# A retention block on one core: earlier loads of the first value weights and of the second chunk's values, another layout of the retention tiles, and another place for some gate products and transpositions

## The chip, the core and the metric

The program runs on one core of a Trainium2 chip. A core has a matrix engine (PE; its weight loads are shown apart as PEld), a vector engine (DVE), a scalar engine (ACT), a general engine (POOL) and a sequencer that issues transfers (SP). Each engine takes its instructions in the order of the program, and waits at semaphores for what other engines or transfers have to deliver. The metric is the device time in microseconds (us) of one execution; smaller is better. All times below are us unless ns is written.

## What is computed

One hybrid decoder block on 1024 tokens of width 1024, batch 1, in float32:

```python
h = modulate(rms_norm(x, norm1_g), sh1, sc1)
proj = h @ w_in                  # retention q, k, v, gate; attention q, k, v; two merge gates
rq, rk = rotary(rq), rotary(rk) * 256 ** -0.5
def step(state, inp):            # retention: 4 heads, 8 chunks of 128 tokens, dk 256, dv 512
    qi, ki, vi = inp
    s = einsum('bhid,bhjd->bhij', qi, ki) * inner_decay
    o = einsum('bhij,bhje->bhie', s, vi) + einsum('bhid,bhde->bhie', qi, state) * q_decay
    state = state * chunk_decay + einsum('bhjd,bhje->bhde', ki * k_decay, vi)
    return state, o
ret_out = (silu(rg) * group_norm(ro)) @ w_ret_out
att_out = merge_by_lse(dilated_group(...) for three groups) @ w_att_out
x = x + g1 * ((sigmoid(gate_a) * ret_out + sigmoid(gate_b) * att_out) @ w_o)
x = x + g2 * (square(relu(modulate(rms_norm(x, norm2_g), sh2, sc2) @ w_ff1)) @ w_ff2)
return rms_norm(x, norm_f_g)
```

## The kernel before

Every product of two float32 matrices is made of three passes of a reduced float32 type: an operand is split into a high half (a rounding copy, mostly on ACT) and a low half (the rest, a subtraction on DVE, or on POOL for the retention's queries and keys), and `mm3` (L196) runs low x high, high x low and high x high into one PSUM tile. So what PE multiplies must have been loaded, copied and subtracted before.

The order of the work is written out by hand; the program's order is the order on each engine. Around the change it is this:

* `queries_keys` (L1152) makes 22 pairs of projections. Each pair is seven block products, in the order `11, s1, s3, s2, 12, 22, s4` (L215), of 12 matmuls each. After a product the function `after` (L1167) issues side work. For the last pair it calls `mod_step` (L1284) at `11` and `12`, which ends in a transfer into the `cossin` tile, and `v_load` (L1208), which issues the loads of the weights of the values' first two products: the first product's after `12`, the second's after `s4`. After `22` it splits the first product's weights: `v_w` (L1215) copies on ACT, `v_low` (L1221) subtracts on DVE.
* `values` (L1291) makes the retention's values in 14 products of four parts each, and writes them to DRAM (`v_d`). Near its end it fetches queries, keys and values of the first chunks, and `first["release"]` lets the weight loader of the steps (`Steps.run`, L71) go on; that loader keeps up to three raw weight tiles (`wraw`, three buffers, tag `raw`) ahead and stops at a mark (`Steps.mark`, L63). Up to here tiles live in the pool `xpool`: 26 buffers of 4 KB for each partition, taken in turn.
* `open_ret` (L520) closes `xpool` and opens the pool `ret` on the same memory. Its tiles are laid out in the order in which their tags are first used: five small tiles (4.5 KB together), `state`, `stateh`, `statel` (4 KB each), four buffers `V` of 4 KB, four buffers `qk` of 2 KB, small ones, three buffers `j` of 4 KB, and so on. A tile's first write waits until the last use of the old tile in the same place is over.
* `chunk` (L723) is one of 32 retention steps, g = 8 h + c. On PE it runs the state's outer product `kv` (6 matmuls), one gate product (`gates`, 6 matmuls of 512 columns, from `rg` weights; not in chunks with c % 4 = 0), the next chunk's scores and transposed keys `s_kt` (L634), the output `o` (3 or 9 matmuls), the transposition `on_T` (L673) of the normalised output of two chunks ago, and the remaining gate products. At the start of chunks with c % 4 = 0 ACT applies `silu` (L719) to the gate of the four chunks before, and then splits queries and keys (`jit_qk`, L623). `s_halves` (L651) copies (ACT) and subtracts (DVE) the transposed keys, `kh` and `kl`; `state` is updated on DVE (L764, L766), its high half `stateh` copied on ACT (L781), its low half `statel` made on DVE (L801). `fetch(g + 3)` at the head of the chunk issues the transfers of queries, keys and values three chunks ahead. PSUM tiles come from two rings: `mm` with two buffers (the gate's sum holds one for four chunks) and `s` with four.

The transfers named here are all issued by SP, in program order, and one that has to wait holds up those behind it. POOL issues its own (`h12d`, L1321 and L1322).

Of the kernel before, what the change touches and what calls it, by code (L numbers as in the profile page):

```python
# [17 lines left out]
P = 128  # L18
# [115 lines left out]
def block_kernel(ctx, tc, io, stop=None, dbg=None):  # L134
# [385 lines left out]
    def open_ret():  # L520
        x_ctx.close()
        R["p"] = ret_ctx.enter_context(tc.tile_pool(name="ret", bufs=1, reuse_waits="tile"))
        for n in R_SMALL:
            R[n] = r_small(n, "00")
        R["state"] = R["p"].tile([P, 2, DV], F32, name="state")
        R["sh"] = R["p"].tile([P, 2, DV], F32R, name="stateh")
        R["sl"] = R["p"].tile([P, 2, DV], F32R, name="statel")
# [4 lines left out]
    def r_small(n, name):  # L532

        if n in R:
            return R.pop(n)
        shape, dt, bufs = R_SMALL[n]
        return R["p"].tile(shape, dt, tag=n, bufs=bufs, name=n + name)

    def etile(name, dt=F32):
        return R["p"].tile([P, 1024], dt, tag="E", bufs=11, name=name)  # L540
# [57 lines left out]
    qk_d = [dram.tile([P, 4, S], F32, name=f"qkd{h}") for h in range(H)]  # L598
    v_d = [dram.tile([P, NC, 2, DV], F32, name=f"vd{h}") for h in range(H)]

    def fetch(i):

        h, c = divmod(i, NC)
        if i > 1:
            hd["qk", i] = R["p"].tile([P, 4, C], F32, tag="qk", bufs=4, name=f"qk{h}{c}")
        elif i == 0:
            t = whl.tile([P, 1024], F32, tag="wl", name="qk01").rearrange("p (a b c) -> p a b c", a=2, b=4)
            for j in range(2):
                hd["qk", j] = t[:, j]
                nc.sync.dma_start(t[:, j], qk_d[0][:, :, j * C:(j + 1) * C])  # L610
        if i > 1:
            nc.sync.dma_start(hd["qk", i], qk_d[h][:, :, c * C:(c + 1) * C])
        if i > 0:
            v = R["p"].tile([P, 2, DV], F32R, tag="V", bufs=4, name=f"v{h}{c}")
        else:
            v = whl.tile([P, 1024], F32R, tag="wh", name="v00").rearrange("p (a b) -> p a b", a=2)
        hd["v", i] = v
        nc.sync.dma_start(fv(v), v_d[h][:, c])

# [3 lines left out]
    def jit_qk(i):  # L623
        src = hd["qk", i]
        if i > 1:
            t = R["p"].tile([P, 2, 4, C], F32R, tag="j", bufs=3, name=f"j{i}")
        else:
            t = whl.tile([P, 1024], F32R, tag=("wh", "wl")[i], name=f"j{i}")
            t = t.rearrange("p (a b c) -> p a b c", a=2, b=4)
        nc.scalar.copy(t[:, 0], src)  # L630
        nc.gpsimd.tensor_sub(t[:, 1], src, fv(t[:, 0]))  # L631
        hd["j", i] = t
# [90 lines left out]
    def chunk(h, c, ahead, w=None):  # L723
        p = R["p"]
        g = NC * h + c
        if g + 3 < NG:
            fetch(g + 3)
        if w:
            hd["w"] = w
        if c in (6, 7):  # L730
            hd["srg", h, c - 4] = etile(f"srg{h}{c - 4}")
            nc.sync.dma_start(hd["srg", h, c - 4], srg_d[h][c - 6])
        if c % 4 == 0:
            if g > 0:
                silu(*divmod(g // 4 - 1, 2))
            hd["rgw"] = hd.pop("w")
            hd["rgp"] = ps_mm(f"rg{h}{c}")
        ks = ((0, 1, 2, 3), (4, 5), (6,), (7,))[c] if g < 4 else range(2 * (c % 4), 2 * (c % 4) + 2)
        early = int(c % 4 > 0)
        gated = h > 0 and 1 < c < 6  # L740

        def gates(ks):
            proj_mm(hd["rgp"], hd["rgw"], ks, (1, 3, 5, 7, 0, 2, 4, 6))

        if g == 0:
            gates(ks[:2])
            s_kt(0)
            s_halves(0)()()
            gates(ks[2:])
        elif g + 2 < NG:  # L750
            jit_qk(g + 2)
        if gated:
            u_scaled(h - 1, c - 2)
        vh, vl = hd["v", g][:, 0], hd["v", g][:, 1]
        st, sh, sl = R["state"], R["sh"], R["sl"]
        if c < NC - 1:
            kh, kl = hd["k", g]
            kv = ps_mm(f"kv{h}{c}")
            for i in range(2):
                mm3([kv[:, i]], (kh[:, i, :], kl[:, i, :]), [(vh, vl)], True, True)  # L760
        if g > 0:
            gates(ks[:early])
        if c == 0:
            nc.vector.tensor_copy(flat(st), flat(kv))  # L764
        elif c < NC - 1:
            nc.vector.scalar_tensor_tensor(flat(st), flat(st), float(GAMMA[h] ** C), flat(kv),  # L766
                                           op0=ALU.mult, op1=ALU.add)
        if g > 0:
            norm_bias(g - 1)
        high = low = None  # L770
        if g + 1 < NG:
            s_kt(g + 1)
            high = s_halves(g + 1)
        po = ps_s(f"o{h}{c}")
        if c > 0:
            t = hd["j", g]
            for i in range(2):
                mm3([po], (t[:, 0, i, :], t[:, 1, i, :]), [(sh[:, i, :], sl[:, i, :])], i == 0, False)
        mm3([po], hd["s", g], [(vh, vl)], c == 0, True)
        if c < NC - 1:  # L780
            nc.scalar.copy(flat(sh), flat(kv if c == 0 else st))  # L781
        if g > 0:
            normed(g - 1)
        if high:
            low = high()
        if g > 1:
            on_T(*divmod(g - 2, NC))
        if g > 0:
            gates(ks[early:])
        bn = p.tile([P, 6], F32, tag="bn", bufs=2, name=f"bn{h}{c}")  # L790
        ba = p.tile([P, 2], F32, tag="ba", bufs=2, name=f"ba{h}{c}")
        gr = p.tile([P, 1], F32, tag="gr", bufs=2, name=f"gr{h}{c}")
        nc.vector.bn_stats(bn, po)
        nc.vector.bn_aggr(ba, bn)
        nc.vector.tensor_add(gr, ba[:, 1:2], ct[:, CS_EPS + h:CS_EPS + h + 1])
        nc.gpsimd.tensor_tensor(gr, gr, mhalf[:, 0:1], op=ALU.pow)
        hd["o", h, c] = po, ba, gr
        if low:
            low()
        if c < NC - 1:  # L800
            nc.vector.tensor_sub(flat(sl), flat(st), fv(flat(sh)))  # L801
        ahead(2)
        if gated:
            u_gated(h - 1, c - 2)
        if g == 0:
            jit_qk(g + 2)
        if g == NG - 1:
            norm_bias(g)
            normed(g)
            silu(h, 1)  # L810

    def wsplit(ap):
        return ap, split_w
# [338 lines left out]
    def queries_keys(ahead):  # L1152
        for _ in range(4):
            copy_block()
        gn_signs()
        sums = [(q, n) for q in range(NA) for n in ORDER][4:]
        while len(BA.slots) > 1:
            BA.prep(sums.pop(0))

        def before(q, n):  # L1160
            if n == ORDER[0] and q + 2 < NA:
                for part in (1, 2):
                    a_load(q + 2, part)

        turns = []

        def after(q, n):  # L1167
            if n in ("s1", "s2", "12"):
                copy_block()
            if n == "11" and 0 < q < 4:  # L1170
                bias_out(q - 1)
            if turns:
                next(turns[0], None)
            if (q, n) == (NA - 6, "22"):
                mod_fetch(0)
                mod_fetch(1)
            if q >= NA - 5 and n in ("11", "12"):
                mod_step()
            if n == ORDER[-1] and PAIRS[q][0] == "r":
                while turns:  # L1180
                    drain(turns.pop())
                turns.append(rotate(q))
            if q == NA - 1 and n in ("12", "s4"):
                v_load(n == "s4")
            if q == NA - 1 and n == "22":
                for j in range(2):
                    v_w(0, j)
                for j in range(2):
                    v_low(0, j)

        BA.run([(q, n) for q in range(NA) for n in ORDER], sums, before, after)
        while turns:
            drain(turns.pop())
        values(ahead)


# [83 lines left out]
    def mod_fetch(i):  # L1280
        if i < len(later_mods):
            nc.sync.dma_start(cs[:, i % 2], io["w_ada"][later_mods[i]])
# [8 lines left out]
    def values(ahead):  # L1291
        last = len(VSEQ) - 1
        for i, (hp, n) in enumerate(VSEQ):
            if i + 2 <= last:
                v_load(i + 2)
            for p in range(4):
# [12 lines left out]
                    mod_step()  # L1309

                if i == last - 2 and p == 2:
                    fetch(0)
                if i == last - 2 and p == 3:
                    first["release"]()
                if i == last - 1 and p in (1, 2):
                    jit_qk(p - 1)
                if i == last - 1 and p == 3:
# [4 lines left out]
                        nc.gpsimd.dma_start(hl[2 * m][:, 512:], h12_d[m][:, 1])  # L1322
        v_post(*V["post"].pop())
        open_ret()
        for g in (1, 2):
            fetch(g)
        banks(False)

    for kk in range(4):
# [9 lines left out]
    for h in range(H):  # L1339
        for c in range(NC):  # L1340
            steps.add((lambda h, c: lambda ahead, *w: chunk(h, c, ahead, *w))(h, c),
                      [wsplit(w) for w in r_loads.get((h, c), ())], manual=True)


    A = {}
# [1339 lines left out]
```

## Time and profile before

| quantity | value |
|---|---|
| median of 3 runs | 2212.76 us (2210.62 to 2216.35) |
| profiled execution | 2214.49 us, span of its trace 2212.6 us |
| PE busy | 2157.9 us, 98% of the span, 10034 matmuls |
| DVE, ACT, POOL busy | 1472.7, 944.8, 169.2 us |
| 568.60 to 725.00, values: PE busy | 154.02 of 156.40 us |
| 725.40 to 960.00, retention: PE busy | 227.64 of 234.60 us |

The profile is one execution. A busy time is the time in which an engine has an instruction under way; idle time ahead of an instruction is put down to what ended last before it started. Positions are us from the start of the span. In the timeline a row is: start, length, engine, line, operation, output<-inputs, shape, count, and in brackets the idle time before it with what ended it. PE's matmul rows overlap: a matmul of 512 columns takes 0.39 us, and the next starts some 0.23 us after it.

### The profile page before, as it was taken

The numbers are of one execution on the slowest core, as the hardware profiler recorded it, in microseconds if no ns is written. First come the engines' busy times: TensorE is split into PE (matmuls) and PEld (weight loads), VectorE is DVE, ScalarE is ACT, GpSimd is POOL, SyncE is SP. The second block draws the span as 40 slices with busy tenths as digits, with TensorE's granted clock in tenths as the row PEclk, the third lists the DMA queues.
The fourth block names the chain that finished last, engine by engine and source line by source line (L and its number), as shares of the span: only waits on it lengthen the run. The fifth ranks groups of instructions, "written<-read, shape, count | busy, mean of one in ns | idle before, by whom it ended". The sixth has DMA issues, their size and how long they took to land.

```text
span 2212.6 us, 27000 instructions
## 1 busy us (share of the span) xinstructions
PE 2157.9 (98%) x10034; PEld 1787.3 (81%) x10034; DVE 1472.7 (67%) x2271; ACT 944.8 (43%) x1709; POOL 169.2 (8%) x176
## 2 busy tenths in 40 slices
PE   7999999999999999999899999999999999999998
PEld 4888888888788788888788788888878888788887
DVE  6756777766566677754555644676876665787855
ACT  4532323333234466654534634524454445533412
POOL 0100111000001233300000000002100000000003
PEclk9999999999999999999999999999999999999999
DMA  9869999744687645569523265654154445645322
GB/s 383 222 208 294 293 304 278 200 153 151 222 298 289 227 158 190 176 216 259 166 79 105 87 214 186 238 179 164 38 191 148 147 147 183 250 135 175 119 86 77
DMA packets 159906, 422.54 MB, mean 191 GB/s; under 512 B 27478, under 2 KB 55389, under 8 KB 155358
## 3 DMA queue, kind: packets, MB, share of 16 engines
q1 hardware_dynamic: 151902, 372.57, 47.5%
q0 software_dynamic: 7872, 48.24, 9.4%
q8 instruction: 79, 1.29, 0.2%
q14 instruction: 53, 0.43, 0.1%
HBM read 325.71 MB, written 160.32 MB: 220 GB/s over the span
## 4 chain that ended last, share of the span: by engine, by line
PE 85%; DVE 6%; ACT 4%; DMA 3%; issue 1%; POOL 0%; SPq 0%; POOLq 0%; DVEq 0%; ACTq 0%
PE qap L200 6%; PE qap L204 6%; PE qap L202 6%; PE fp L200 4%; PE fp L202 4%; PE fp L204 4%; PE f2a L202 2%; PE f2a L204 2%; PE f2a L200 2%; PE ak L200 2%; PE ak L202 2%; PE ak L204 2%; PE va L202 1%; PE va L204 1%; PE va L200 1%; PE rg L202 1%
## 5 line engine op out<-in xcount | busy, mean ns | idle before, releaser
L200 PE MATMUL qap<-hh,qaw 128*128 128x512 f32 x264 | 102.9, 390 | 0.2 <-DVE qat L291 0.2
L202 PE MATMUL qap<-hl,qaw 128*128 128x512 f32 x264 | 102.7, 389 | 0.0
L204 PE MATMUL qap<-hh,qaw 128*128 128x512 f32 x264 | 102.7, 389 | 0.0
L631 POOL TENSOR_TENSOR j<-qk,j 128x512 fp32r<-128x512 f32 x32 | 50.5, 1579 | 326.4 <-ACT j L630 326.4
L2140 ACT ACTIVATE a<-a 128x512 f32<-128x512 f32 x48 | 30.3, 632 | 79.3 <-DVE a L2139 79.3
L2036 POOL TENSOR_TENSOR accnf<-accnf,sqnf 128x256 f32<-128x256 f32 (+1 forms) x18 | 16.6, 922 | 613.3 <-ACT sqnf L2035 613.3
L1492 ACT ACTIVATE P<-P,ng 128x128 f32<-128x128 f32 (+1 forms) x96 | 41.9, 438 | 41.5 <-DVE ng L1489 41.5
L200 PEld LDWEIGHTS qap<-hh,qaw 128*128 128x128 f32 x264 | 49.6, 188 | 11.1 <-DVE qat L291 0.9
L204 PEld LDWEIGHTS qap<-hh,qaw 128*128 128x128 f32 x264 | 49.6, 188 | 10.4
L202 PEld LDWEIGHTS qap<-hl,qaw 128*128 128x128 f32 x264 | 49.6, 188 | 10.3
L2329 ACT CAST w2h<-w2s 128x512 fp32r<-128x512 f32 x36 | 22.4, 622 | 79.0 <-DVE w2s L2367 79.0
L257 DVE TENSOR_TENSOR fw<-w1r,fw 128x512 fp32r<-128x512 f32 x48 | 32.9, 688 | 33.3 <-ACT fw L247 33.3
L257 DVE TENSOR_TENSOR qaw<-wa,qaw 128x512 fp32r<-128x512 f32 x66 | 45.1, 687 | 12.6 <-ACT qaw L247 12.6
L2036 POOL TENSOR_TENSOR accn<-accn,sqn 128x512 f32<-128x512 f32 x12 | 15.6, 1296 | 488.6 <-ACT sqn L2035 488.6
L247 ACT CAST qaw<-wa 128x512 fp32r<-128x512 f32 x66 | 39.8, 617 | 25.3 <-PE qap L204 15.2
L200 PE MATMUL fp<-h2h,fw 128*128 128x512 f32 x128 | 50.0, 390 | 0.0
L204 PE MATMUL fp<-h2h,fw 128*128 128x512 f32 x128 | 49.8, 389 | 0.0
L202 PE MATMUL fp<-h2l,fw 128*128 128x512 f32 x128 | 49.8, 389 | 0.0
L200 PE MATMUL roa<-rh,rwl 128*128 128x512 f32 x128 | 49.8, 389 | 0.0
L202 PE MATMUL roa<-rl,rwh 128*128 128x512 f32 x128 | 49.8, 389 | 0.0
L204 PE MATMUL roa<-rh,rwh 128*128 128x512 f32 x128 | 49.8, 389 | 0.0
L1874 DVE TENSOR_TENSOR rwl<-rwl,rwh 128x1024 fp32r<-128x1024 f32 x25 | 30.2, 1221 | 29.0 <-ACT rwh L1904 29.0
(3057 smaller groups left out, 7126.3 us busy)
## 6 DMA issues: line engine op xcount, KB each, us to landing
cossin<-in_w_ada_dram SPq DMA_DIRECT2D x32, 512.0 KB, 5.1
v<-vd SPq DMA_DIRECT2D x32, 512.0 KB, 4.7
w1r<-in_w_ff_dram SPq DMA_DIRECT2D x32, 512.0 KB, 4.8
vd<-vo SPq DMA_DIRECT2D x24, 512.0 KB, 6.6
yt<-y POOLq DMA_DIRECT2D x6, 2048.0 KB, 15.0
xsd<-as SPq DMA_DIRECT2D x24, 512.0 KB, 3.0
w2r<-in_w_ff2s_dram SPq DMA_DIRECT2D x24, 512.0 KB, 7.6
em<-in_w_ada_dram SPq DMA_DIRECT2D x16, 512.0 KB, 10.2
```

The costliest lines, as they stand in the source:

```text
L200: nc.tensor.matmul(o, wl, xh, start=first, stop=False, skip_group_check=skip)
L202: nc.tensor.matmul(o, wh, xl, start=False, stop=False, skip_group_check=skip)
L204: nc.tensor.matmul(o, wh, xh, start=False, stop=last, skip_group_check=skip)
L247: nc.scalar.copy(t[:, :512], src)
L257: nc.vector.tensor_sub(t[:, 512:], src, fv(t[:, :512]))
L631: nc.gpsimd.tensor_sub(t[:, 1], src, fv(t[:, 0]))
L1492: nc.scalar.activation(v, v, AF.Exp, bias=ng[:, blk:blk + 1], accum_out=st[:, g, blk, 2 + a:3 + a])
L1874: nc.vector.tensor_sub(lo, fv(lo), fv(hi))
L2036: (nc.vector if f == 7 else nc.gpsimd).tensor_add(G["acc", key], G["acc", key], sq)
L2140: nc.scalar.activation(o, o, AF.Relu)
L2329: nc.scalar.copy(hi, src)
```

## The change

Six edits, all around the values and the retention:

1. `v_load` of the first value product moves from behind `12` of the last pair to behind `s1`; that of the second from behind `s4` to behind `12`.
2. `fetch` is split into `fetch_qk` and `fetch_v`. The second chunk's values go into a buffer of `wraw` and are fetched in `values`, right behind the release of the weight loader, and no longer behind `open_ret`. A new mark makes that release stop after two gate weights; a third release at the head of chunk 2 lets the loader go on.
3. Queries and keys are fetched four chunks ahead, values three as before.
4. In `open_ret` a `j` tile is the first tile of the pool, so that the three `j` buffers lie in front and everything else moves up by 12 KB; `qk` now comes ahead of `V`.
5. In chunk 0 the four gate products run one ahead of `s_kt(0)`, one behind it and two behind `o`, in place of two and two.
6. In the chunks with c % 4 = 0 the two gate products at the end run ahead of the transposition, and no longer behind it.

```diff
     def open_ret():
...
+        R["j"] = j_tile(2)
         for n in R_SMALL:
...
+    def j_tile(i):
+        return R["p"].tile([P, 2, 4, C], F32R, tag="j", bufs=3, name=f"j{i}")
...
-    def fetch(i):
+    def fetch_qk(i):
 
         h, c = divmod(i, NC)
         if i > 1:
             hd["qk", i] = R["p"].tile([P, 4, C], F32, tag="qk", bufs=4, name=f"qk{h}{c}")
+            nc.sync.dma_start(hd["qk", i], qk_d[h][:, :, c * C:(c + 1) * C])
...
+    def fetch_v(i):
+
+        h, c = divmod(i, NC)
         if i > 1:
-            nc.sync.dma_start(hd["qk", i], qk_d[h][:, :, c * C:(c + 1) * C])
-        if i > 0:
             v = R["p"].tile([P, 2, DV], F32R, tag="V", bufs=4, name=f"v{h}{c}")
         else:
-            v = whl.tile([P, 1024], F32R, tag="wh", name="v00").rearrange("p (a b) -> p a b", a=2)
+            pool, tag = ((whl, "wh"), (wraw, "raw"))[i]
+            v = pool.tile([P, 1024], F32R, tag=tag, name=f"v0{i}").rearrange("p (a b) -> p a b", a=2)
...
     def jit_qk(i):
         src = hd["qk", i]
         if i > 1:
-            t = R["p"].tile([P, 2, 4, C], F32R, tag="j", bufs=3, name=f"j{i}")
+            t = R.pop("j") if "j" in R else j_tile(i)
...
         if g + 3 < NG:
-            fetch(g + 3)
+            fetch_v(g + 3)
+        if g + 4 < NG:
+            fetch_qk(g + 4)
+        if g == 2:
+            first["release"]()
...
         if g == 0:
-            gates(ks[:2])
+            gates(ks[:1])
             s_kt(0)
             s_halves(0)()()
-            gates(ks[2:])
+            gates(ks[1:2])
...
-        if g > 0:
-            gates(ks[:early])
+        gates(ks[:early])
...
         if high:
             low = high()
+        if c % 4 == 0:
+            gates(ks[early if g else 2:])
         if g > 1:
             on_T(*divmod(g - 2, NC))
-        if g > 0:
+        if c % 4:
             gates(ks[early:])
...
+            if q == NA - 1 and n in ("s1", "12"):
+                v_load(n == "12")
...
-            if q == NA - 1 and n in ("12", "s4"):
-                v_load(n == "s4")
...
                 if i == last - 2 and p == 2:
-                    fetch(0)
+                    fetch_qk(0)
+                    fetch_v(0)
                 if i == last - 2 and p == 3:
                     first["release"]()
+                    fetch_v(1)
...
         open_ret()
-        for g in (1, 2):
-            fetch(g)
+        fetch_qk(2)
+        fetch_v(2)
+        fetch_qk(3)
         banks(False)
...
+            if h == 0 and c == 2:
+                steps.mark()
```

## The prediction

> **What bounds the kernel now.** First the page's head and its busy times, then the waits of PE, then the stages in which these waits lie.
>
> ```profile
> span 2212.6 us, 27000 instructions
> ...
> PE 2157.9 (98%) x10034; PEld 1787.3 (81%) x10034; DVE 1472.7 (67%) x2271; ACT 944.8 (43%) x1709; POOL 169.2 (8%) x176
> ```
>
> PE is busy for 98% of the span, so time can only be won where PE waits, or where its clock is down. The view of the waits of PE, by the instruction that waited, has these rows in the stretch that the change touches (total us, times, longest):
>
> ```profile
> PE oT L680 <- DVE kl L660: 4.1, 4, 1.8
> ...
> PE kv L200 <- DMA v<-vd: 2.8, 1, 2.8
> ...
> PE va L200 <- ACT vwh L1217: 1.6, 1, 1.6
> ...
> PE va L202 <- DVE vwlFalse L1224: 0.8, 1, 0.8
> ```
>
> The view of the windows gives the granted clock (third number from the end):
>
> ```profile
> 560.00:565.00 5.00, 5.00 (x24) 4.14 (x23) 3.81 (x6) 0.60 (x1) 0.00 (x0) 1.00 0.01 3
> 571.60:575.50 3.90, 3.90 (x10) 3.03 (x11) 2.22 (x2) 0.74 (x1) 0.00 (x0) 0.56 0.07 28
> 732.00:734.00 2.00, 2.00 (x14) 1.74 (x12) 0.93 (x1) 0.22 (x1) 0.00 (x0) 1.00 0.04 13
> 1063.60:1070.40 6.80, 3.02 (x8) 2.34 (x9) 3.57 (x8) 6.77 (x10) 0.00 (x0) 0.50 0.89 208
> ...
> 1275.20:1278.60 3.40, 3.40 (x12) 2.92 (x12) 2.04 (x1) 0.18 (x1) 0.00 (x0) 0.50 0.01 5
> 1623.40:1630.20 6.80, 5.73 (x14) 4.47 (x15) 5.58 (x10) 4.43 (x8) 0.00 (x0) 0.50 0.48 177
> ```
>
> Behind the waits at the first value product the clock fell to 0.56 over 3.90 us: 3.90 x 0.44 = 1.7 us lost besides the waiting. Three later places lose 3.4, 1.7 and 3.4 us in the same way.
>
> **First weights sooner (edit 1).** The boundary between the last projection pair and the values, from the timelines of PE, ACT, DVE and SP (`vwlFalse` are the first product's weights, `vwlTrue` the second's):
>
> ```profile
> 568.31 0.39 PE L204 MATMUL qap<-hh,qaw21s 128*128 128x512 f32 x1
> 570.32 0.50 PE L200 MATMUL va<-vwh,hl 128*128 128x512 f32 x1 [1.62 <-ACT vwh L1217]
> 563.35 0.60 ACT L1117 ACTIVATE qa<-qap 128x512 f32<-128x512 f32 x1 [10.30 <-PE qap L204]
> 569.21 1.06 ACT L1217 ACTIVATE vwh<-vwlFalse 128x1024 fp32r<-128x1024 f32 x1 [5.26 <-DMA vwlFalse<-wrv]
> 580.20 1.06 ACT L1217 ACTIVATE vwh<-vwlTrue 128x1024 fp32r<-128x1024 f32 x1 [7.86 <-DMA vwlTrue<-wrv]
> 566.02 1.12 DVE L1119 TENSOR_TENSOR qa<-qap,qat 128x512 f32<-128x512 f32 x1 [1.47 <-PE qap L204]
> 570.30 1.23 DVE L1224 TENSOR_TENSOR vwlFalse<-vwlFalse,vwh 128x1024 fp32r<-128x1024 f32 x1 [3.16 <-ACT vwh L1217]
> 551.56 13.15 SPq L1282 DMA_DIRECT2D cossin<-in_w_ada_dram  x2
> 564.81 0.86 SPq L1213 DMA_DIRECT2D vwlFalse<-wrv  x2
> 567.17 7.81 SPq L1131 DMA_DIRECT2D aqd<-qa  x2
> 575.07 1.22 SPq L1213 DMA_DIRECT2D vwlTrue<-wrv  x2
> ```
>
> The load is issued at 564.81, behind the second `cossin` transfer, and ACT has it at 569.21, 4.4 us later. Issued behind `s1` it stands between the two `cossin` transfers and can leave near 552, if its buffers are free; they are those that the pool would have given to the pair's results. At the pace of the row it is there before 559, and ACT is free at 563.35 + 0.60 = 563.95: two copies of 1.06 end at 566.1. DVE is held until 567.14 by L1119, then needs 1.23 for each low half: 568.4 and 569.6. PE ends the pair at 568.54, wants the first low half one matmul later and the second after six (569.9). So both waits go, 1.62 + 0.76 (0.8 in the waits); each also let PE drain, since a matmul lasts 0.39 but is followed after 0.23 (twelve in 2.72, next fence), 0.16 each; and the 1.7 of the clock. Gain: 2.4 + 0.3 + 1.7 = **4.4 us**. If the buffers come free late, 0 is the other bound; I take 4.4 because the slack in the load is 5 us.
>
> The second product's loads leave at 575.07, behind `aqd`, which waits for DVE, and are split from 580.20. With the values 4.4 us sooner the first product (48 matmuls of 0.227 = 10.9 us) ends at 568.54 + 10.9 = 579.4, and PE would wait 3 us for that second split. Moved ahead of `aqd`, they leave near 565, land by 573 (even at 8 us), and cost nothing: that is the cover for this half of the edit. `aqd` gets 1.2 us behind it on SP and nobody waits for it before the attention.
>
> **Second chunk's values, layout, spread gate products (edits 2, 4, 5).** Rows of PE, DVE and SP:
>
> ```profile
> 725.39 0.61 PE L200 MATMUL rg<-hh,raw_5287l 128*128 128x512 f32 x2
> 728.11 0.28 PE L642 MATMUL sT<-j 128*128 128x256 f32 x1
> 728.67 0.71 PE L200 MATMUL rg<-hh,raw_5287l 128*128 128x512 f32 x2
> 733.98 0.40 PE L204 MATMUL o<-v,smh 128*128 128x512 f32 x1
> 737.16 0.47 PE L200 MATMUL kv<-v,kl 128*128 128x512 f32 x1 [2.78 <-DMA v<-vd]
> 729.52 0.48 DVE L660 SCALAR_TENSOR_TENSOR kl<-kT,ct,kh 128x256 fp32r<-128x256 f32 x1 [1.85 <-ACT kh L659]
> 733.07 1.23 DVE L764 COPY state<-kv 128x1024 f32<-128x1024 f32 x1 [1.90 <-PE kv L204]
> 704.36 2.18 SPq L84 DMA_DIRECT2D raw<-in_w_rg_dram  x3
> 719.53 8.48 SPq L1267 DMA_DIRECT2D vd<-vr  x4
> 733.55 0.32 SPq L618 DMA_DIRECT2D v<-vd  x1
> 780.22 1.22 DVE L191 TENSOR_TENSOR raw_5291l<-raw,raw_5291h 128x1024 fp32r<-128x1024 f32 x1 [0.19 <-ACT raw_5291h L190]
> ```
>
> Two gate products take 728.11 - 725.39 = 2.72, one 1.36; `s_kt` 0.56; `kv`, six matmuls too, 1.36; `o` of chunk 0 0.68. The chunk's work is unchanged in sum. In the new order: gate to 726.75, `s_kt(0)` to 727.31, gate to 728.67. `kl` ended at 730.00, 1.89 behind the start of `s_kt`, so now at 728.64: just in time for `kv` at 728.67 (a spread that cost more would be seen here; up to 0.2). Then `kv`, `s_kt(1)`, `o`, two gates: chunk 1's `kv` is reached at 728.67 + 1.36 + 0.56 + 0.68 + 2.72 = 734.0, and its values now leave SP near 706, in the place of the third `raw` of the row at 704.36. Gain up to 737.16 - 734.0 = 3.1.
>
> But the wait behind the old 733.55 has not gone. The values' transfer stood at the end of the last `vd<-vr` (8.48 from 719.53), with the transfer engines at 13 GB/s by 732-734: it waited for the old tile in its place to be written out. Before, `V` began at 4.5 + 3 x 4 = 16.5 KB; now the three `j` (12 KB) and the small tiles (4.5 KB) put `state` at 16.5 KB, the same place, with `stateh` behind it. So what is late next is DVE's L764, and behind it on DVE `kl` of chunk 1: 733.55 + 1.23 + 0.48 = 735.3, gain 1.9. On ACT `stateh` waits alike, and `jit_qk(2)` behind it; `s_kt(2)` is reached 2.7 us after `kv`, enough for 0.6 on ACT and 1.3 on POOL. One transfer of 512 KB fewer stands ahead of that landing, so it may come a microsecond sooner, or, with queries and values now issued at 728 beside it, some 3 us later (gain -1). Bounds -1 and 3.1; I take **2.3 us**, near the row's 1.9.
>
> The release's mark moves that third gate-weight load and the one behind it to chunk 2, near 744; the third is split at 780.22, so over 30 us cover it. Queries one chunk sooner use buffers last read a chunk earlier, and hide behind everything; three `j`, four `qk` and four `V` remain.
>
> **Transpositions behind the gate products (edit 6).** The four waits of 4.1 us lie at chunks 4, 8, 16 and 24. Chunk 4 from the timelines, and ACT's groups in the retention:
>
> ```profile
> 760.14 0.40 PE L204 MATMUL o<-v,smh 128*128 128x512 f32 x1
> 761.35 0.33 PE L680 MATMUL oT<-ct,onm 128*128 128x128 f32 x1 [0.82 <-DVE kl L660]
> 758.87 1.03 ACT L721 ACTIVATE srg<-rg 128x1024 f32<-128x1024 f32 x1
> L682 ACT COPY on<-oT 128x128 f32<-128x128 f32 x120 | 23.3, 282 | 7.1 <-DVE on L694 6.4 <-PE oT L680 0.7
> L630 ACT CAST j<-qk 128x512 fp32r<-128x512 f32 x30 | 19.0, 634 | 8.1 <-DMA qk<-qkd 8.0
> L689 ACT ACTIVATE on<-on,gnt 128x512 f32<-128x512 f32 x24 | 18.3, 816 | 0.0
> ```
>
> The transposition needs the PSUM buffer that `kl` still reads, and `kl` is late because `silu` stands ahead of it on ACT. Two gate products (2.72) now run in between, more than the longest wait (1.8). They need the `mm` buffer that `silu` reads: free at 759.90, PE there at 760.54. Gain: 4.1 + 4 x 0.16 = **4.8 us**. ACT's copies of the transposition come 2.72 later; behind them wait four copies (1.13), `j` (0.63), and in chunk 5 of a head two L689 (1.63), 3.4 together, while PE needs 1.36 + 1.36 + 0.56 = 3.3 and 0.3 more before the next `kh`: hidden, narrowly.
>
> **Sum.** 4.4 + 2.3 + 4.8 = 11.5 us. The profiled execution took 2214.49 (span 2212.6 and 1.9 around it): 2203.0. It lies 1.7 over the median of the runs shown, about one fall of the clock; from the median it is 2201.3. I predict **2202**.
>
> [...]
>
> **Rivals.** *The clock falls elsewhere* (0.16): everything behind 960 shifts by 11.5 us, and whether a wait lowers the clock depends on more than its length, since the rows above show one fall or two. Two falls more or fewer are 2 x 1.7: 2205.4 or 2198.6. *A wait only moves* (0.10): the transposition still waits behind the gates, or `state` is held for 3 us: 4.8 lost, 2206.8. For it: that landing is unknown; against it: the margins above. *The gain is lost in the attention* (0.05): its waits grow by what was won, 2214.49 - 1.7 = 2212.8. For it: the transfers at 1063.60 (208 GB/s beside a PE busy for 3.02 of 6.80); against it: what they bring is asked for by PE's own progress. *Slower* (0.03): ACT's queue. If the work behind the late copies does not fit, each of the seven chunks 4 to 28 loses up to 2.72: 19.0, 2202 + 19 = 2221. It decides once that work lasts 11.5 / 7 = 1.6 us over the 3.6 that are free; the groups give 3.4.
>
> **Chances.** The forecast has 0.66, with its own range 2199 to 2205. A measurement of this kernel can tell about 0.3%, 6.6 us: faster is below 2206.1, slower above 2219.4. Faster: 0.65 of the forecast, 0.14 of the first rival, 0.03 of the second, 0.82. Slower 0.04, the rest 0.14. The range takes in both signs of the clock and the moved wait: 2197 to 2208.
>
> **What would show it.** No wait of PE at the first `va`, and clock 1.00 there; chunk 1's `kv` 1 to 3 us behind `o` and gates, its wait on DVE; `state<-kv` idle before it on a `vd` transfer; no wait at `oT` in chunks 4, 8, 16, 24. I am wrong if `oT` waits as before, if the first weights leave SP near 564 again, or if waits behind 960 grow by as much.

## The result, and the profile after

The changed kernel takes 2200.71 us (median of 5 runs, 2196.09 to 2206.35) against 2212.76 (5 runs, 2210.62 to 2216.35): the ratio is 0.9943, with a 95% interval from 0.9919 to 0.9966. The forecast was 2202. The profiled execution took 2196.09, the lowest of the five. Its page begins so:

```profile
span 2194.1 us, 26997 instructions
...
PE 2151.7 (98%) x10034; PEld 1784.1 (81%) x10034; DVE 1472.7 (67%) x2271; ACT 944.5 (43%) x1709; POOL 166.4 (8%) x176
```

PE has the same 10034 matmuls. The four rows of PE's waits that the prediction began with (`va` twice, `kv`, `oT`) have no counterpart in the view after. The windows (stretch; its length; busy time of PE, PEld, DVE, ACT and POOL with instructions; clock; DMA share; GB/s) show PE busy all through the two places:

```profile
571.60:575.50 3.90, 3.90 (x19) 3.24 (x18) 2.42 (x3) 2.13 (x3) 0.00 (x0) 1.00 0.90 279
721.00:731.00 10.00, 10.00 (x52) 8.34 (x51) 7.10 (x16) 3.99 (x9) 1.10 (x2) 1.00 1.02 358
...
1608.24:1611.65 3.41, 3.41 (x10) 2.64 (x9) 2.74 (x5) 3.09 (x6) 0.00 (x0) 0.50 0.11 38
```

The last row is the only stretch at half clock between the start and the last six microseconds: 3.4 us, where the execution profiled before had windows of 3.4, 6.8, 3.4 and 6.8 us by the exact edges, 20.5 together. At the clock of 0.50 matmuls of 512 columns start 0.43 us apart (572.18 to 575.17 in the execution before) in place of 0.23, so about half the time is lost at most: by that estimate at most (20.5 - 3.4) / 2 = 8.5 of the 18.4 us between the two profiled executions are the clock's, up to 1.7 of them at the first value product.

The stretches that the change touches can be read directly. From the last matmul of the pair (568.31 before, 569.04 after) to the first gate product of the retention (725.39, 721.59) PE took 157.08 us before and 152.55 after; from there to the attention's first scores (970.36, 958.48) 244.97 and 236.89. That is 4.5 + 8.1 = 12.6 us, of which at most 1.7 are the clock's. The other 5.8 lie outside these stretches: three falls of the clock behind them against one, and one wait at a gate product of the attention of 3.8 us before and 1.6 after. The medians, 12.05 us apart, hold less of that.

The boundary after, from the timelines of PE, ACT, DVE and SP (start; duration; engine; line; operation):

```profile
569.04 0.39 PE L204 MATMUL qap<-hh,qaw21s 128*128 128x512 f32 x1
569.27 0.39 PE L200 MATMUL va<-vwh,hl 128*128 128x512 f32 x1
564.52 2.00 ACT L1230 ACTIVATE vwh<-vwlFalse 128x1024 fp32r<-128x1024 f32 x2
567.82 2.35 DVE L1237 TENSOR_TENSOR vwlFalse<-vwlFalse,vwh 128x1024 fp32r<-128x1024 f32 x2
552.72 1.26 SPq L1226 DMA_DIRECT2D vwlFalse<-wrv  x2
554.02 0.91 SPq L1226 DMA_DIRECT2D vwlTrue<-wrv  x2
565.11 0.33 SPq L1295 DMA_DIRECT2D cossin<-in_w_ada_dram  x1
```

Both products' loads left before the second `cossin`; the copies and low halves were done in time, and PE went from the pair to the values in one matmul's distance, 0.23.

The start of the retention, from the same timelines:

```profile
721.59 0.62 PE L200 MATMUL rg<-hh,raw_5287l 128*128 128x512 f32 x2
726.93 0.48 PE L200 MATMUL o<-v,sml 128*128 128x512 f32 x1
730.02 0.62 PE L204 MATMUL rg<-hh,raw_5287h 128*128 128x512 f32 x2
730.47 0.39 PE L200 MATMUL kv<-v,kl 128*128 128x512 f32 x1
726.58 1.23 DVE L775 COPY state<-kv 128x1024 f32<-128x1024 f32 x1 [0.57 <-PE kv L204]
715.73 8.48 SPq L1280 DMA_DIRECT2D vd<-vr  x4
```

From the first gate product to chunk 1's `kv` PE took 730.47 - 721.59 = 8.88 us, before 737.16 - 725.39 = 11.77: 2.9 won, near the upper bound of 3.1. But DVE's copy into `state` waited for PE's `kv` alone and not for a `vd` transfer, which the prediction named, and chunk 1's `kv` did not wait at all.

At the transpositions, chunk 8 for one, PE ran on (the rows of the four chunks are alike):

```profile
779.56 0.40 PE L204 MATMUL o<-v,smh 128*128 128x512 f32 x1
779.80 0.62 PE L200 MATMUL rg<-hh,raw_5638l 128*128 128x512 f32 x2
...
782.10 0.62 PE L204 MATMUL rg<-hh,raw_5638h 128*128 128x512 f32 x2
782.55 0.60 PE L688 MATMUL oT<-ct,onm 128*128 128x128 f32 x4
```

### The profile page after: what moved, and what is told of

It reads as the page before. It is cut to its first block, busy times and chain, and to the rows that moved or that the text cites. A ratio compares the mean times of both kernels' runs of the same rounds, so it can differ in the third digit from the quotient of the medians.

```text
span 2194.1 us, 26997 instructions
## 1 busy us (share of the span) xinstructions
PE 2151.7 (98%) x10034; PEld 1784.1 (81%) x10034; DVE 1472.7 (67%) x2271; ACT 944.5 (43%) x1709; POOL 166.4 (8%) x176
## 4 chain that ended last, share of the span: by engine, by line
PE 84%; DVE 7%; ACT 4%; DMA 3%; issue 1%; SPq 0%; POOL 0%; POOLq 0%; DVEq 0%; ACTq 0%
PE qap L200 6%; PE qap L204 6%; PE qap L202 6%; PE fp L200 4%; PE fp L202 4%; PE fp L204 4%; PE f2a L202 2%; PE f2a L204 2%; PE f2a L200 2%; PE ak L200 1%; PE ak L202 1%; PE ak L204 1%; PE rg L202 1%; PE rg L200 1%; PE rg L204 1%; PE va L204 1%
## 5 line engine op out<-in xcount | busy, mean ns | idle before, releaser
L200 PEld LDWEIGHTS qap<-hh,qaw 128*128 128x128 f32 x264 | 49.5, 188 | 11.5 <-DVE qat L291 1.4
L257 DVE TENSOR_TENSOR qaw<-wa,qaw 128x512 fp32r<-128x512 f32 x66 | 45.0, 686 | 12.7 <-ACT qaw L247 12.6
L1288 DVE SCALAR_TENSOR_TENSOR cossin<-cossin,cb 128x1024 f32<-128x1024 f32 x32 | 39.0, 1219 | 15.9 <-DMA cossin<-in_w_ada_dram 15.9
## 6 DMA issues: line engine op xcount, KB each, us to landing
em<-in_w_ada_dram SPq DMA_DIRECT2D x16, 512.0 KB, 10.2
```

Of the source, the lines that this page charges most:

```text
L200: nc.tensor.matmul(o, wl, xh, start=first, stop=False, skip_group_check=skip)
L257: nc.vector.tensor_sub(t[:, 512:], src, fv(t[:, :512]))
L1288: nc.vector.scalar_tensor_tensor(t, t, 1.0, cb, op0=ALU.mult, op1=ALU.mult, accum_out=mods[:, j:j + 1])
```

## The experiments

Theory: the three groups of edits remove three waits, each worth what the wait was, and the rest is cover. The rivals: a part does nothing, or does its work through something else, above all through where the last result tile of the values (`vr`) lies. All were run beside the kernel before; since a fall of the clock more or less moves an execution by up to 1.7 us for each 3.41 us at 0.50, the verdict on a part is read from PE's waits, in one profiled execution each. By the times alone no part taken back lies clear of the changed kernel: the intervals all touch or overlap that of changed_again. "Excess" is the distance between two matmuls beyond the usual one of their form, so it holds the wait and the drain of PE.

| run | median us | ratio to before, 95% interval | excess at the places in question |
|---|---|---|---|
| changed_again | 2196.07 | 0.9944 [0.9931, 0.9957] | none |
| first_loads_back | 2199.01 | 0.9949 [0.9937, 0.9961] | `va` 1.68 + 1.03, `sT` of chunk 2 0.47 |
| second_load_back | 2198.25 | 0.9944 [0.9932, 0.9957] | none |
| values_back | 2196.67 | 0.9939 [0.9927, 0.9951] | none |
| layout_back | 2202.04 | 0.9969 [0.9957, 0.9981] | `kv` of chunk 0 3.33 |
| spread_back | 2197.87 | 0.9953 [0.9940, 0.9966] | `kv` of chunk 1 1.19, `sT` of chunk 2 0.58 |
| transpose_first | 2201.84 | 0.9968 [0.9955, 0.9980] | `oT` 0.97 + 0.92 + 0.92 + 0.93 |
| queries_transpose_back | 2201.49 | 0.9961 [0.9949, 0.9973] | `oT` 0.95 + 0.92 + 0.91 + 0.82 |
| fewest_parts | 2196.93 | 0.9942 [0.9928, 0.9956] | none |
| before_first_loads | 2207.90 | 0.9992 [0.9983, 1.0000] | `kv` of chunk 0 2.68, of chunk 1 0.81, `sT` 0.64; `oT` as before |
| before_transpose_behind | 2206.50 | 0.9987 [0.9977, 0.9998] | `va` 2.01 + 1.03, `kv` of chunk 1 2.68 |

The kernel before took 2208.72 to 2209.97 in these sets.

### changed_again

> The changed kernel once more, beside the parts that are taken back. Its ratio to the kernel before should be that of its first measurement, 0.992 to 0.997, and its profile has no wait at va, kv of chunk 1 and oT. Where the profiled execution differs from the first one, theory: only in falls of the clock and in the waits beside them; rival: other waits of PE come and go too.

It held: 13 us below the kernel before, and no wait at the three places. The profiled execution had three falls of the clock (13.7 us at half clock, 0.996 on average over the span) where the first had one (3.4 us, 0.998), and the wait at a gate product of the attention was 2.2 us in place of 1.6 (3.8 in the kernel before).

### first_loads_back: edit 1 taken back

```diff
-            if q == NA - 1 and n in ("s1", "12"):
-                v_load(n == "12")
...
+            if q == NA - 1 and n in ("12", "s4"):
+                v_load(n == "s4")
```

> The changed kernel with edit 1 alone taken back: both products' first value weights are loaded in their old places again, behind 12 and s4; all else stays. Theory: PE waits again at the first va, 1.6 us on ACT's high half and 0.8 us on DVE's low half, with a clock of 0.5 for about 3.4 us behind it in some executions; with the drain of PE that is 2.7 us, 4.4 us where the clock falls. A second effect is to be seen if edit 1 also moved the place of the last result tile of the values (vr of the last block): in this kernel that tile lies under state and stateh, so DVE's copy into state should wait for the landing of the last vd transfer, about 4.4 us after its issue, some 1.7 us longer than in the changed kernel; PE's kv of chunk 1 then stands at most 0.9 us later. Rival: the new layout alone freed state of that wait, and DVE's copy waits for PE's kv only, as in the changed kernel (0.57 us). Time by the theory 2.7 to 5.3 us above the changed kernel.

Two of PE's waits, then rows of DVE, ACT and PE at the start of the retention:

```profile
PE va L200 <- ACT vwh L1230: 1.5, 1, 1.5
...
PE va L202 <- DVE vwlFalse L1237: 0.8, 1, 0.8
```

```profile
724.07 0.61 PE L200 MATMUL rg<-hh,raw_5287l 128*128 128x512 f32 x2
...
730.41 1.22 DVE L775 COPY state<-kv 128x1024 f32<-128x1024 f32 x1 [1.92 <-PE o L204]
731.67 1.01 ACT L792 CAST stateh<-kv 128x1024 fp32r<-128x1024 f32 x1 [1.29 <-DVE state L775]
732.93 0.39 PE L200 MATMUL kv<-v,kl 128*128 128x512 f32 x1
736.12 0.39 PE L650 MATMUL sT<-j 128*128 128x256 f32 x1 [0.30 <-POOL j L639]
```

Both effects are there. The waits at `va` are back, 2.7 us with the drain. And DVE's copy into `state` is idle for 1.92 in place of 0.57: it names PE's `o`, but `kv` had long been done; the last `vd<-vr`, issued at 726.36, landed by the trace at 730.29, and the copy began 0.12 later. So with edit 1 gone `state` does lie on the last result tile, and the prediction's wait exists. It costs little: `kv` of chunk 1 starts 732.93 - 724.07 = 8.86 us behind the first gate product, as in the changed kernel; only `j`, queued on ACT behind the late `stateh`, makes PE wait 0.3 (0.47 with the drain) at `sT` of chunk 2.

### second_load_back: the second product's weights loaded in their old place

```diff
-            if q == NA - 1 and n in ("s1", "12"):
-                v_load(n == "12")
+            if q == NA - 1 and n == "s1":
+                v_load(0)
...
+            if q == NA - 1 and n == "s4":
+                v_load(1)
```

> The changed kernel with the second product's weights loaded behind s4 again, as before the change; the first product's stay early. By the prediction PE would wait 3 us at the second product. By the profile of the changed kernel less: there SP is done with aqd at 571.68, the first of the two loads would land 5.7 to 6.9 us later, near 577.9, its copy (1.06) and low half (1.22) would end at 580.2, just when the first product of 48 x 0.227 = 10.9 us is over (569.27 + 10.9 = 580.2); the second tile 1 to 2 us later, needed 1.4 us later. So 0 to 1 us of waiting, and no fall of the clock. Time 0 to 1 us above the changed kernel by the profile, 3 to 5 us by the prediction.

Rows of SP, ACT and DVE (the tile has the name `vwl` here):

```profile
572.78 1.20 SPq L1228 DMA_DIRECT2D vwl<-wrv  x2
578.18 1.06 ACT L1232 ACTIVATE vwh<-vwl 128x1024 fp32r<-128x1024 f32 x1 [10.54 <-DMA vwl<-wrv]
579.27 1.22 DVE L1239 TENSOR_TENSOR vwl<-vwl,vwh 128x1024 fp32r<-128x1024 f32 x1 [6.96 <-ACT vwh L1232]
```

No wait. The prediction's 3 us fall: it kept the landing of before (580.20), but with DVE done sooner, `aqd` no longer holds SP until 575.07; the load left 2.3 us sooner.

### values_back: chunk 1's values back in the retention's pool

```diff
-        if i > 1:
+        if i > 0:
             v = R["p"].tile([P, 2, DV], F32R, tag="V", ...)
...
-                    fetch_v(1)
...
         open_ret()
+        fetch_v(1)
         fetch_qk(2)
```

> The changed kernel with chunk 1's values back in the retention's own V tile, so that their load is issued only after the pools have changed, behind the last vd transfer on SP. Theory A (the earlier load won the gain): PE waits for them at kv of chunk 1, as before the change, 1 to 3 us. Theory B (the gain came from where the last result tile lies: no tile that is written early in the retention stands on it any more, so SP doesn't hold the load back): the load leaves SP near 724.4, lands near 729 and is there before kv of chunk 1 at 730.5; no wait. By A the time is 1 to 3 us above the changed kernel, by B the same.

```profile
724.62 0.38 SPq L625 DMA_DIRECT2D v<-vd  x1
```

```profile
730.78 0.39 PE L200 MATMUL kv<-v,kl 128*128 128x512 f32 x1
```

Theory B holds: the load left SP right behind the last `vd` (before it was held until 733.55), landed by the trace at 729.39, and PE took it at 730.78 with no wait. Beside edits 1 and 4, loading these values sooner gained nothing.

### layout_back: the old order of the retention's tiles

```diff
         R["p"] = ret_ctx.enter_context(...)
-        R["j"] = j_tile(2)
...
-            t = R.pop("j") if "j" in R else j_tile(i)
+            t = j_tile(i)
```

> The changed kernel without edit 4: the retention's tiles in their old order, the small ones first and j after them. By its addresses the small tiles (sm, kh, kl, smh) and the first part of sml then lie on the last result tile of the values, which the last vd transfer still reads. Theory: ACT's first kh of the retention waits for that landing, which came 6.7 us after the first gate product in the changed kernel; its copy and the low half take 0.5 and 0.5 us more, so kv of chunk 0 starts 7.6 to 8.2 us behind the first gate product in place of 3.4: PE waits 4.2 to 4.8 us, and the clock falls to 0.5 behind it (up to 1.7 us more). Rival: the layout alone is worth nothing, kh waits only for PE's kT, no wait. Time 4 to 6.5 us above the changed kernel by the theory, the same by the rival.

The first copy of the retention on ACT, the wait of PE, and the windows of 3.413 us around it:

```profile
730.75 0.47 ACT L666 ACTIVATE kh<-kT,ct 128x256 fp32r<-128x256 f32 x1 [4.13 <-DMA vd<-vr]
```

```profile
PE kv L200 <- DVE kl L667: 3.2, 1, 3.2
```

```profile
727.33:730.74 3.41, 1.30 (x6) 0.73 (x4) 0.01 (x1) 0.00 (x0) 0.00 (x0) 1.00 0.91 317
730.74:734.16 3.42, 2.36 (x6) 1.88 (x7) 1.26 (x4) 0.93 (x3) 0.00 (x0) 0.50 0.98 313
734.16:737.57 3.41, 3.41 (x13) 2.93 (x12) 2.24 (x5) 1.55 (x4) 0.00 (x0) 0.50 1.05 365
```

The theory's wait, with its releaser named: ACT waits for the `vd` transfer, PE 3.2 us behind it (the landing came sooner than assumed, 3.3 us after its issue), and the clock is at half for two windows. The run is some 6 us above the changed kernel. What the layout does is to put `j` of chunk 2, which is written late, on the tile that is read out last: in the changed kernel ACT writes it from 729.09 on, and the last `vd` had landed by the trace at 728.28.

### spread_back: chunk 0's gate products two and two again

```diff
-            gates(ks[:1])
+            gates(ks[:2])
             s_kt(0)
             s_halves(0)()()
-            gates(ks[1:2])
+            gates(ks[2:])
...
-        if c % 4 == 0:
-            gates(ks[early if g else 2:])
+        if g > 0 and c % 4 == 0:
+            gates(ks[early:])
```

> The changed kernel with edit 5 taken back: chunk 0's four gate products stand two ahead of its s_kt and two ahead of its kv again, and none behind its o. Theory: kv of chunk 1 then comes 0.68 us behind kv of chunk 0 and the 0.56 of s_kt, while DVE needs 1.23 for state and 0.48 for kl after kv of chunk 0 ends: kv of chunk 0 ends near 7.4 us behind the first gate product, kl of chunk 1 near 9.4 and kv would start at 8.6 to 8.9. PE waits 0.5 to 0.8 us at kv of chunk 1. Rival: kl is ahead of PE there too, no wait. Time 0.5 to 1 us above the changed kernel by the theory, the same by the rival.

```profile
731.96 0.50 PE L200 MATMUL kv<-v,kl 128*128 128x512 f32 x1 [1.02 <-ACT stateh L792]
735.41 0.39 PE L650 MATMUL sT<-j 128*128 128x256 f32 x1 [0.42 <-POOL j L639]
```

A wait there is, but it is not `kl`'s: that was done at 730.85 + 0.48 = 731.33. PE waited for ACT's copy out of chunk 0's `kv` (730.90 + 1.01 = 731.91). With the wait at `sT` of chunk 2 behind it, the spread is worth 1.19 + 0.58 = 1.8 us by the waits; the medians differ by as much.

### transpose_first and queries_transpose_back: edit 6 taken back, then edit 3 too

```diff
-        if c % 4 == 0:
-            gates(ks[early if g else 2:])
+        if g == 0:
+            gates(ks[2:])
         if g > 1:
             on_T(*divmod(g - 2, NC))
-        if c % 4:
+        if g > 0:
             gates(ks[early:])
```

> The changed kernel with edit 6 taken back: the transpositions of chunks 4, 8, 12 and so on stand ahead of the second gate products again. Theory: the waits at oT of chunks 4, 8, 16 and 24 return with their sizes of before, 0.8, 0.8, 0.7 and 1.8 us (4.1 together), 4.8 us with the drain. Rival: the wait of chunk 24 (1.8 us) came from queries that were loaded late, behind a weight load on SP, and edit 3 loads them one chunk sooner: then only three waits of 0.8 us return, 2.3 us together, 2.8 us with the drain. Time 4.8 us above the changed kernel by the theory, 2.8 by the rival.

The second run adds this to the first:

```diff
+            fetch_qk(g + 3)
             fetch_v(g + 3)
-        if g + 4 < NG:
-            fetch_qk(g + 4)
...
         fetch_v(2)
-        fetch_qk(3)
```

> The changed kernel with edit 6 and edit 3 taken back: the transpositions stand ahead of the second gate products, and the queries are loaded three chunks ahead in place of four. With edit 6 alone taken back the wait of chunk 24 was 0.75 us, against 1.8 in the kernel before. Theory: the other 1.05 us are edit 3's: with the queries loaded late again, ACT's j of chunk 26 waits for them at chunk 24 behind the weight load that holds SP, kl comes late, and the wait at oT of chunk 24 is 1.3 to 1.8 us; chunks 4, 8 and 16 keep 0.75 to 0.8. Rival: the size of that wait is chance, and it is 0.75 here as in the other three. Time 4 to 5 us above the changed kernel by the theory, 3.5 to 4 by the rival.

The wait of PE in the first:

```profile
PE oT L688 <- DVE kl L668: 3.1, 4, 0.8
```

and in the second, with the row of ACT at chunk 24:

```profile
PE oT L688 <- DVE kl L668: 2.9, 4, 0.8
```

```profile
892.60 0.62 ACT L638 CAST j<-qk 128x512 fp32r<-128x512 f32 x1 [0.73 <-DMA qk<-qkd]
```

Neither theory nor rival of the first run holds: all four waits return, each 0.75 to 0.8, so edit 6 is worth 3.7 us with the drain here, not 4.8. (The medians are 5.8 us apart, 2201.84 against 2196.07, more than these waits.) The second run doesn't bring the 1.8 of chunk 24 back: ACT does wait for the late queries again, 0.73 (in the execution before 1.89), but PE's wait there is 0.65. In before_first_loads it was 1.26. How long those queries take varies between executions; the 1.05 us beyond the other three waits is not a fixed price, and what edit 3 gains on average stays open.

### before_transpose_behind: edit 6 alone on the kernel before

```diff
+        if g > 0 and c % 4 == 0:
+            gates(ks[early:])
         if g > 1:
             on_T(*divmod(g - 2, NC))
-        if g > 0:
+        if c % 4:
             gates(ks[early:])
```

> The kernel before with edit 6 alone: at chunks 4, 8, 12 and so on the second gate products stand ahead of the transpositions. Theory: the four waits at oT (4.1 us, 4.8 with the drain) are gone and nothing takes their place; the waits at the first va (2.4) and at chunk 1's values (2.8) stay. Time 4 to 5 us below the kernel before. Rival: ACT's work behind the late copies of the transposition makes kh or j late, and new waits of PE appear in the chunks behind 4, 8, 16 and 24; the time is less than 3 us below.

No wait at `oT` is left, and none of 0.3 us or more has come up in chunks 4 to 31: the rival falls, and with it the prediction's slower case. From the first gate product (725.61) to the attention's first scores (965.35) PE took 239.74 us against 244.97 before: 5.2 less, 0.3 of them at `kv` of chunk 1, where the excess was 2.95 before. The medians lie only 2.2 us apart, where the rival had put the time; their interval, 0.4 to 5 us, can't decide between that and the 4 to 5 expected, so the waits do.

### before_first_loads: edit 1 alone on the kernel before

The diff is that of first_loads_back, the other way round.

> The kernel before with edit 1 alone: both products' first value weights loaded sooner, nothing else. By its addresses the last result tile of the values then lies under the small tiles of the retention (sm, kh, kl, smh) and no longer under chunk 1's values. Theory (the place decides): no wait at the first va (2.4 us won, 2.7 with the drain, 4.4 where the clock fell); no wait at chunk 1's values; but ACT's first kh waits for the landing of the last vd transfer, near 6.7 us behind the first gate product, and kv of chunk 0, wanted 6.0 us behind it, starts at 7.6 to 8.2: 1.6 to 2.2 us of waiting there, and 0.5 to 0.8 at kv of chunk 1 for kl. Rival (only the load's time counts): the wait of 2.8 us at chunk 1's values stays and kv of chunk 0 does not wait. Both give about the same time, 3 to 5 us below the kernel before; the waits tell them apart.

```profile
728.36 0.47 ACT L659 ACTIVATE kh<-kT,ct 128x256 fp32r<-128x256 f32 x1 [6.22 <-DMA vd<-vr]
```

```profile
PE kv L200 <- DVE kl L660: 2.5, 1, 2.5
...
PE kv L200 <- ACT stateh L781: 0.4, 1, 0.4
```

```profile
727.05:730.46 3.41, 1.05 (x5) 0.87 (x6) 1.19 (x4) 0.93 (x3) 0.00 (x0) 1.00 1.10 377
730.46:733.88 3.42, 3.42 (x12) 2.47 (x10) 1.91 (x4) 1.12 (x3) 0.00 (x0) 0.50 1.02 356
```

The place decides: the waits at `va` and for chunk 1's values are gone, and ACT's first `kh` waits for the `vd` transfer in their stead, PE at chunk 0 behind it. Excess of 2.68 + 0.81 + 0.64 and a fall of the clock eat most of what edit 1 won; the run is 1 us below the kernel before, and not 3 to 5 as both theory and rival had it.

### fewest_parts: without the parts that seemed cover only

It puts the diffs of second_load_back and values_back and the queries' part of queries_transpose_back together.

> A smaller change: the first product's weights sooner (the first half of edit 1), the new layout (edit 4), the spread gate products (edit 5) and the transpositions behind the gates (edit 6); chunk 1's values, the queries and the second product's weights are loaded in their old places. Theory: the other parts only cover what no longer waits, so there is no wait of 0.3 us or more at va, kv of chunk 1 and oT, and the time is that of the changed kernel within 2 us. Rival: SP, with these loads back in its queue behind the last vd transfer, brings chunk 1's values or the queries of chunk 2 and 3 late; PE waits 0.5 to 2 us in chunks 1 to 3.

As the theory has it: no such wait, and 2196.93 us against 2196.07 of changed_again. Half of edit 1 and edits 4, 5 and 6 carry the measured gain.

### first_loads_back_2: the clock

> The kernel of the first experiment (edit 1 taken back) once more, for the clock. In the profiles so far the granted clock changes only on a grid of 3.413 us, and falls to 0.5 where PE was idle for 1.97 us or more of the window before, never where it was idle for 1.80 or less (with one fall at 0.91). Theory: so it will be here: the waits at the first va, 1.5 and 0.75 us, lower the clock if one window holds 1.97 us or more of them, and do not if the grid's edge parts them. Rival: length of the wait decides, or chance: a fall with the wait parted in two, or none with the wait in one window.

Windows of 3.413 us on the grid of the clock's changes, first_loads_back, then its second execution:

```profile
566.48:569.89 3.41, 2.18 (x10) 1.48 (x8) 0.62 (x1) 0.82 (x1) 0.00 (x0) 1.00 1.02 377
569.89:573.30 3.41, 2.26 (x8) 1.34 (x8) 2.60 (x3) 1.30 (x2) 0.00 (x0) 1.00 0.45 179
573.30:576.72 3.42, 3.42 (x15) 2.82 (x16) 0.92 (x1) 0.00 (x0) 0.00 (x0) 1.00 0.48 160
```

```profile
569.15:572.56 3.41, 1.10 (x4) 0.37 (x2) 1.23 (x1) 1.26 (x2) 0.00 (x0) 1.00 0.94 345
572.56:575.98 3.42, 3.37 (x8) 2.73 (x9) 2.23 (x2) 0.86 (x1) 0.00 (x0) 0.50 0.05 22
```

The same two waits: where the grid parted them (idle 3.41 - 2.18 = 1.23 and 1.15) the clock stayed at 1.00, where one window held both (3.41 - 1.10 = 2.31) the next was at 0.50. The theory holds in this one execution more (2198.97 us).

## Why the prediction was right, and where not

*The first weights.* Right: no wait at the first `va`, and 2.7 us of waiting with the drain, as the sum had it (first_loads_back). The 1.7 of the clock is a chance, not a sum: with these waits in place it fell in three of four profiled executions (before, before_transpose_behind, first_loads_back_2; not in first_loads_back). In these four it went with where the waits lay on the grid of 3.413 us: behind 2.38, 1.94 and 2.31 us of idle time in one window the next was at 0.50, behind 1.23 and 1.15 in two windows the clock stayed at 1.00. The sum took the price as certain. The loads left at 552.72 as forecast, the second product's at 554.02 and not near 565, since no `cossin` stood between. That this half is cover for a wait of 3 us was wrong: without it PE does not wait (second_load_back).

*The second chunk's values.* The size came out (2.3 forecast, 2.9 measured, bound 3.1), the reason did not. The step that failed is "put `state` at 16.5 KB, the same place". It reckoned where the retention's tiles move and took the result tile to stay. Edit 1 takes two buffers of the pool earlier, and by the addresses of the compiled kernels, which no profile shows, the last result tile then comes to lie at the pool's start: under `j` in the new layout, under `kh` in the old one. What the profiles show is who waits for its transfer: chunk 1's values in the kernel before; `kh` with edit 1 and the old layout (before_first_loads, layout_back); `state` with the new layout and no edit 1 (first_loads_back), the forecast wait, which even there costs 0.47 and not 1.2; and nobody with both. Why edit 1 moves the tile is argued and not shown. So edits 1 and 4 belong together: one moves the tile, the other sees that what is written last lies on it. Edit 2, which the step gave the gain to, gains nothing beside them (values_back). The spread, to which the prediction gave no gain of its own and a cost of up to 0.2, is worth 1.8 by the waits (spread_back). So that the forecast of 2.3 lies near 2.9 is in part luck.

*The transpositions.* The mechanism was right, on ACT too: behind the gates the transposition waits for nothing, and the copies that come later delay nobody. The 4.8 us were one execution's: with the queries fetched three chunks ahead the four waits made 4.8, 4.5 (before_first_loads) and 3.6 us with the drain (queries_transpose_back), with four chunks 3.7 (transpose_first). Three waits of some 0.8 repeat; the one of chunk 24 was 1.80, 1.26, 0.65 and 0.76, and the sum took the highest.

*The sum.* By PE's waits the parts are 2.7, 2.9 and 3.6 to 4.8, 9.2 to 10.4 together; forecast were 11.5 - 1.7 = 9.8, and 1.7 for the clock. The clock can be read from all runs, since each lists its granted clock. It is 0.9959 on average in the 50 runs of the kernel before beside the experiments, and 0.9966 to 0.9968 in each of the five sets of runs with none of these waits (the changed kernel twice, second_load_back, values_back, fewest_parts; 28 runs). One minus the clock, times the time, gives 9.0 us lost against 7.3: 1.7 less, give or take 1.1 by the scatter of the runs, and an upper estimate, as PE isn't busy all through these windows (3.02 of 6.80 us at 1063.60, where the prediction counts 3.4 us lost). The mean times are 2209.8 and 2197.9, 11.9 apart, 10.2 of it not the clock's. So the size of both terms came out, the clock's on average and not in each execution. Which falls of the clock went isn't shown: the waits beside them in the attention, too, differ from execution to execution, as the first rival has it. Between single sets the medians differ by 12.05 and 13.0, and by that scatter the 2202 lies closer to 2200.71 than its terms could promise.

## What to carry to other kernels

When a pool is closed and another opened over it, look up which of the new tiles lies on the old tile that is read out last, and put there what is written late; any change of allocation before that point, an earlier load too, may move the old tile, so look it up again for each version. A wait that stands once in one execution is priced from several; of its share, the half clock behind it is a probability (it came in three of four executions here). And take parts back one at a time: three of this change's parts (half of edit 1, edits 2 and 3) could go with no loss that these runs can tell.

## What the runs showed of the hardware

In the traces of the kernel before and of the changed kernel the granted clock is 1.00 or 0.50. It falls at 572.08, 1063.60, 1275.22, 1623.38 and 2207.06 us in the first, at 1608.24 and 2188.51 in the second; the last fall of each lasts to the end of the span, those at 1063.60 and 1623.38 last 6.83 us, the others 3.41. In the first trace all these falls and the rises behind them lie whole multiples of 3.413 us apart, and so do the two falls and the rise of the second. Counted from the start of the span, 572.08 is 167.60 such steps and 1608.24 is 471.16, so the two grids lie differently.

PE's idle time in windows on this grid that ran at 1.00, by the clock of the window behind (from 60 us on in the first two rows, all such windows that were idle for 1.0 us or more or had 0.50 behind them; in the other rows the windows that were viewed at the places above, and one in the attention):

| profile | idle us, then 0.50 | idle us, then 1.00 |
|---|---|---|
| before | 2.38, 2.20, 2.18, 2.10, 0.91 | 1.80, 1.54, 1.48, 1.24, 1.15, 1.10 |
| after | 2.10, 2.05 | 1.59, 1.39, 1.25, 1.16 |
| first_loads_back | | 1.23, 1.15 |
| first_loads_back_2 | 2.31 | |
| before_transpose_behind | 1.94 | 1.80 |
| before_first_loads | 2.36 | 1.80 |
| layout_back | 2.11 | |
| fewest_parts | 0.89 | |

The 0.91 is this window of the kernel before:

```profile
1271.81:1275.23 3.42, 2.51 (x22) 2.28 (x21) 2.25 (x2) 1.05 (x1) 0.00 (x0) 1.00 0.94 351
```

Twenty of its 22 matmuls have 128 columns and start 0.11 us apart, where 512 columns follow each other in 0.227. The 0.89 of fewest_parts is a window with 22 matmuls too, most of them of 128 columns. Why the clock fell behind these two is not shown: no run was made to test it.
